# A GLA head's value projection and part of the modulation put between the level products' steps, with TensorE in source order there

## The chip, the cores and the metric

The kernel runs on one core of one Trainium2 chip, as one launch. The time is the device time of one execution in microseconds; three runs of the kernel before are given, and their median is the number to compare with. The engines are named as in the profile: PE (TensorE, the matrix products), DVE (VectorE), ACT (ScalarE), POOL (GpSimd) and SP (SyncE, which issues most DMAs). Each engine takes its own instructions strictly in the order in which the program lists them, and waits for the others by semaphores.

## The reference, cut to what matters

The reference is a trunk of four layers over 512 latent tokens and 256 context tokens with 1024 features. Each layer makes shift, scale and gate from a conditioning vector (the modulation, `s @ w_mod[i] + b_mod[i]`, 3072 columns), norms its tokens, runs a mixer, and adds the gated, normed result. Layers 0 and 3 have the mixer that the change touches, gated linear attention (GLA) with four heads, key width 128 and value width 256, in both directions:

```
for i in range(DEPTH):                       # kinds: GLA, window attention, RG-LRU, GLA
    shift, scale, gate = split(silu(c) @ w_mod[i] + b_mod[i], 3)
    h = rmsnorm(x, g_pre[i]) * (1 + scale) + shift
    q, k, v, z = split(h @ a_w_in[j])        # per head: 128, 128, 256, 256 columns
    # log gates of every token from a low-rank product; decays between tokens
    o = gla_bidir(q, k, v, la_f, la_b, s_f, s_b)
    y = (rmsnorm_head(o) * silu(z)) @ a_w_out[j]
    x = x + gate * rmsnorm(y, g_post[i])
```

Layer 3 leaves the context's output out, so its heads have fewer tokens in q, z and o.

## The kernel before, in words

Every fp32 product is made of three products of operands split in a high and a low part. Products of 256 or 512 columns run in PE back to back; their weights come in blocks of 256 columns through two 512 KB buffers (`raw`), which the modulation's weights use too, are split by ACT (L243) and by DVE or POOL (L246), and are one block ahead of their use (`weights`).

One GLA head goes through these steps in `gla`:

- `gates(h)`: four small products (L954) and then a chain on ACT and DVE (L958 to L970) that ends in `tmp` and `ls`, the exponentials of the gates' sums over blocks of 1, 2, 4 to 128 tokens. It needs the two PSUM pairs `sct` that the levels of the head before have used.
- `project(h)`: q and k (L362, 72 or 96 products), put into `q` and `Y` by ACT (L984, L979).
- `outputs` of the head before (`prev`): five steps of the state. `turn` transposes Y on PE (L1108), ACT and DVE split it (L1110, L1111), and `step` multiplies it with v (L1118, six products) and updates two states on DVE (L1131). Then chunk products in pairs (L1146), a norm (L1148 to L1152), and the transposed result (`give`, L1159). `turn`, `step`, `chunk` and `give` share two PSUM banks (`mxt`).
- `levels(h)`: X = tmp * q on DVE (L1012; there is one buffer X, so it waits for the last chunk product of the head before), then seven steps L = 1, 2, 4 to 64. Each step has 32 to 96 small products (L1035), 4 at a time beside each other, and behind them DVE decays halves of X and Y (L1063) and ACT copies parts of Y to K (L1030) for the next step. At the end DVE, ACT and POOL make the two score tiles A from the `sct` pairs (L1074 on).
- `zgates(h - 1)`: the gate z of the head before (L372; 48 products of 128x256 and 48 of 128x512 in layer 0, 48 of 128x512 in layer 3).
- `values(h)`: v in three pieces of 48 products of 128x256 (L349).
- `mods`: parts of the modulation, each a DMA of two `raw` buffers, eight products on PE (L499), and later a last step (L517 or L557).

Outside of a `manual_schedule` a scheduler orders every engine at compile time: each instruction has the priority of its place in the source, and the scheduler takes, by its own estimate of durations, the earliest one in the source that is ready. So what comes late in the source fills the times in which what comes early has to wait. Inside `tc.manual_schedule(engines=...)` the named engines keep the source's order among the instructions written there.

The order of one head in the source is: gates, project with outputs of the head before among it, three mods, levels with the z steps behind its steps 1, 3, 5 and 6, the rest of z, values, two mods.

Of the kernel before, what the change touches and what calls it, by code (L numbers as in the profile page):

```python
# [11 lines left out]
F32R = mybir.dt.float32r  # L12
# [63 lines left out]
def body(ctx: ExitStack, tc: tile.TileContext, I, out, layers=(0, 1, 2, 3)):  # L76
# [28 lines left out]
    @contextmanager  # L105
    def phase(name, single=2, double=2):
        """a phase's own SBUF pool and the PSUM banks that phases share out anew, singly and in pairs"""
        with ExitStack() as st:
            if open_already:
                st.push(open_already.pop())  # L110
            else:
                open_banks(st, name, single, double)
            yield open_pool(st, name, bufs=1)

# [10 lines left out]
    # the first phase's banks are there from the start  # L125
# [26 lines left out]
    # the RG-LRU's small parameters  # L152
# [7 lines left out]
    def lru_parameters(bank):  # L160
# [10 lines left out]
        # half biases for the gates' tanh form of the sigmoid  # L171
        V.tensor_scalar(hb, ps[:, 50:90], 0.5, None, op0=ALU.mult)
        # softplus(-lam) = max(-lam, 0) + ln(1 + exp(-|lam|)), times -4 and 2
# [13 lines left out]
    class Mixed:  # L187
        """the mixer's output, features on the partitions; its last two chunks' room is free for
        other use until they are written"""
# [31 lines left out]
    def loadw(pieces):  # L221
        """256 columns; what is returned takes them apart once they are there"""
        rs = []
        for k0 in range(0, KC, 4):
            r = raw()
            for src, o, n in pieces:
                nc.sync.dma_start(
                    r[:, :, o : o + n],
                    src[k0 * P : (k0 + 4) * P, :].rearrange("(k p) n -> p k n", p=P),
                )  # L230
            rs.append(r)

        def convert():
            wh = wp.tile([P, KC, 256], F32R, name="wh", tag="wh")
            wl = wp.tile([P, KC, 256], F32R, name="wl", tag="wl")
            for k0, r in zip((0, 4), rs):
                split(wh[:, k0 : k0 + 4, :], wl[:, k0 : k0 + 4, :], r)
            return wh, wl

        return convert  # L240
# [7 lines left out]
    def load_g1(a):  # L248
        """the low-rank gate projection, both directions, four times over along the columns"""
# [19 lines left out]
    def load_g2(a, zero=True, load=True):  # L269
        """three times over, each direction's rows against its own columns; gpt is free for it"""  # L270
# [16 lines left out]
    def plan(i):  # L287
        """the layer's weight blocks in the order of use"""
# [46 lines left out]
    def weights(key, ahead=True):  # L335
        """the next weight block, with the one after it on its way"""
# [7 lines left out]
    def passes(ps, a, b, kc):  # L344
        """ps += a^T b for pairs (hi, lo) of operand getters over the contraction chunks."""
# [8 lines left out]
    # products begun ahead of their use: the bank's part, and how many tokens of it are done  # L354
    begun = {}

    def ws_part(w, c0, ps, t0, n):
        """128 output columns on the partitions, tokens along the free axis"""
# [8 lines left out]
    def product_steps(ps, w, c0, t0, n):  # L367
        """the same, one product at a time; yields what each takes"""
# [9 lines left out]
    def ws(w, c0, stream):  # L378
        """128 output columns for all tokens of the stream"""
# [8 lines left out]
    def ws_ctx(w):  # L388
        """the context's tokens for both halves of the columns, in one bank but for what was begun elsewhere"""
# [11 lines left out]
    def begin(stream):  # L401
        """the first 256 tokens of what the next weight block brings first"""
# [11 lines left out]
    def ts(wk, kc, rk, tts, ps=None):  # L414
        """tokens on the partitions, 256 output columns along the free axis, for two token tiles."""
# [15 lines left out]
    def gate(pool, w, c0, stream, dst, parts=1):  # L431
        """dst (128 channels, the stream's tokens) *= silu(z), z a 128-column block of the projection."""
# [3 lines left out]
    def gate_ctx(pool, w, dst):  # L436
        """the same for both of the block's halves"""
        silu_times(pool, ws_ctx(w)[0], dst[:, :, CTX0:])
# [15 lines left out]
    def z_steps(pool, w, c, b, put, streams=("ctx", "lat")):  # L454
        """silu(z) for chunk b of the mixer's output, ahead of the output or behind it; put holds
        the token tiles of which either is there"""
# [48 lines left out]
    def mod_ss(i, n, bank, pool=None, bufs=1):  # L505
        """shift (n 0-3) and scale (n 4-7) of layer i, with the features on the partitions; in three steps."""
# [28 lines left out]
    def mod_gate(i, n, bank, pool=None, bufs=1):  # L535
        """gate * g_post of layer i, on all partitions; in three steps."""
# [34 lines left out]
    def background(n):  # L571
        """the next of the modulations; the last step of each comes with the one after it"""
# [20 lines left out]
    def unit_rstd(pool, x, xn):  # L593
        """1 / rms(x); xn is overwritten"""
# [4 lines left out]
    def unit(pool, x, xn):  # L599
        """xn = x / rms(x)"""  # L600
# [3 lines left out]
    def norm_part(pool, i, pr, xn, k, h=None):  # L604
        """xn: token tile -> x / rms(x); writes two chunks of h of layer i, transposed and split, to Rh / Rl."""
# [21 lines left out]
    def first_norm(i):  # L627
        """the same before the first layer, where the modulation comes late: x / rms(x) waits
        transposed in OG, and goes on as its chunks' shift and scale come in. A GLA's first
        products follow chunk by chunk."""  # L630
# [54 lines left out]
        # (two groups share a bank: the first one's first product clears the flags of both)  # L685
# [47 lines left out]
    def finish(i, kc, extra, last, final, xsrc, xdst):  # L733
        """out projection of OG, post norm, residual, and the next layer's pre norm."""
# [3 lines left out]
        with phase(f"fin{i}", 6, 0) as fp:  # L738
# [22 lines left out]
            def product(w, q, tt, ps, k0=0, k1=kc):  # L761
                """a quarter of the columns for a token tile"""
# [10 lines left out]
            def take(q, tt, ps):  # L773
                """quarters 0 and 1, then 2 and 3 at once"""
# [36 lines left out]
            def halves(*parts):  # L811
                """the second half of the columns, a quarter of a token tile at a time"""
# [36 lines left out]
            def chain(tt):  # L849
                """one step of a token tile's way to the next layer's operand at a time"""  # L850
# [64 lines left out]
    def gla(i, a, ctx_out):  # L915
# [3 lines left out]
        with phase(f"gla{i}") as mp:  # L919
# [16 lines left out]
            def gates(h):  # L936
                """exp of the log gates' sums over aligned blocks of 1, 2, .. 128 tokens;
                plane 0 is the backward direction, plane 1 the forward one."""
# [58 lines left out]
            def values(h, v):  # L997
                w = weights(f"v{h}")
                for pr in ((4, 5), (0, 1), (2, 3)):
# [7 lines left out]
            def levels(ls, q, Y, X, A):  # L1007
                """scores inside the 128-token chunks by halving; leaves in X and Y the operands
                decayed to the chunk's edges."""
# [86 lines left out]
            def outputs(h, X, Y, A, v, tl):  # L1096
                gh = mp.tile([P, GDV], F32, name="gh", tag="gh")
                nc.scalar.dma_start(gh, I["a_g_head"][a, h : h + 1].to_broadcast([P, GDV]))
                # the states in front of each chunk, forward (plane 0 of Y) and backward, side by side
# [100 lines left out]
            def mods(n):  # L1200
                for _ in range(n):
                    background(1)
                    yield

# [7 lines left out]
            def among(main, side, every, lead=0):  # L1212
                """steps of main with one of side after some of them; what main leaves of side"""
# [8 lines left out]
            for h in range(GH):  # L1222
# [8 lines left out]
                run(mods(3))  # L1231
                X = mp.tile([P, 2, T], F32, name="X", tag="X")
                A = [mp.tile([P, 6, P], F32R, name=n, tag=n) for n in ("Ah", "Al")]
                lv = levels(ls, q, Y, X, A)
                among(lv, z, [1, 3, 5, 6])
                run(z)
                # the lower part lies where the last head's output goes, but for that head's own
                if h < GH - 1:
                    OG.b = None
                    vl = OG.tail(F32R)  # L1240
                else:
                    vl = mp.tile([P, 2, T], F32R, name="vl", tag="tmp")
                v = (
                    mp.tile([P, 6, GDV], F32R, name="v", tag="v"),
                    vl.rearrange("p d t -> p (d t)").rearrange("p (c n) -> p c n", c=6),
                )
                run(values(h, v))
                run(mods(2))
# [6 lines left out]
    def attention(i):  # L1255
        with phase(f"att{i}", 6, 0) as mp:
# [12 lines left out]
            def rotate(x):  # L1269
                """axial rope on the latent tokens of x (two heads on the partitions), in place."""  # L1270
# [8 lines left out]
            def twice(x, e):  # L1279
                """head e of x on both halves of the partitions"""  # L1280
# [28 lines left out]
            def q_block(kv):  # L1309
                """q of four heads, each head's two parts stacked along the partitions, and their k  # L1310
                in two parts, each of them twice along the partitions"""
# [42 lines left out]
            def fill(ns):  # L1354
                """some of the projections' products, between those of the heads"""
# [13 lines left out]
            def scores(b, qt):  # L1369
# [3 lines left out]
                # local scores in a bank of each head; the context's behind them, in a bank  # L1373
                # of both heads where they do not fit
# [101 lines left out]
            # each unit's scores are a unit ahead of its transposes, two ahead of its output  # L1476
# [23 lines left out]
    def rglru(i, ex, mp):  # L1500
# [33 lines left out]
        def mix(b, up):  # L1534
# [19 lines left out]
            # planes: r', i' of the forward direction, then of the backward one  # L1554
# [24 lines left out]
            for d in range(2):  # L1579
                # sqrt(1 - a^2) = (1 + a) sqrt(tanh(y / 2)) with a = exp(-y)  # L1580
# [11 lines left out]
                # the scan writes over sqrt(1 - a^2), which x holds by now  # L1592
# [99 lines left out]
```

## Time and profile before

| | before |
|---|---|
| three runs, us | 1570.82, 1573.35, 1574.89 |
| median, us | 1573.35 |
| span of the profiled execution, first to last instruction, us | 1568.0 |
| instructions in it | 31484 |
| PE busy | 1489.2 us, 95% |
| DVE busy | 1040.6 us, 66% |
| ACT busy | 774.9 us, 49% |
| POOL busy | 289.1 us, 18% |

Of the profiled execution the profile gives the span, 1568.0 us; it has no time of its own beside that. The median of the three timed runs is 5.35 us above it. A busy time counts the union of an engine's instructions; the products of PE overlap in its pipeline, so a PE that is busy all the time may still have started its products further apart than it could.

GLA takes from 54 us to 377 us (layer 0) and from 1248 us to 1515 us (layer 3) of the span.

### The profile page before, as it was taken

What the parts mean: (1) busy time and instruction counts of PE and PEld (TensorE: products, weight loads), DVE (VectorE), ACT (ScalarE), POOL (GpSimd) and SP (SyncE); (2) the same over time, 40 slices, a digit from 0 to 9 for tenths busy, and PEclk for the clock granted to TensorE, in tenths of its full rate; (3) what the DMA queues carried; (4) which work ended last, traced back from release to release, by engine and by line L of the source; (5) the groups of instructions that cost most, each with busy time, mean ns of one, the idle gap of its engine ahead of it and who ended that gap; (6) DMA issues with size and microseconds to landing.
All of it is one profiled execution on the core that took longest, in us unless ns stands there. A gap on an engine that the chain in (4) does not pass through costs nothing.

```text
span 1568.0 us, 31484 instructions
## 1 busy us (share of the span) xinstructions
PE 1489.2 (95%) x12819; PEld 1279.1 (82%) x12819; DVE 1040.6 (66%) x1918; ACT 774.9 (49%) x1567; POOL 289.1 (18%) x338
## 2 busy tenths in 40 slices
PE   6989999999999999999999999899999999999998
PEld 3777788889987777788789877778899877878888
DVE  5586647575363388787872679989852675776753
ACT  5644343534252376565552556666742545454241
POOL 2221302112121200101001212222311311211211
PEclk8999999999999999999999999999999999999999
DMA  9432324113474532222134633222151243112132
GB/s 306 139 114 78 122 62 132 55 47 130 158 235 133 165 83 58 61 59 55 54 115 143 224 102 114 67 64 61 57 176 44 99 143 98 38 53 68 45 108 81
DMA packets 153057, 162.51 MB, mean 104 GB/s; under 512 B 12418, under 2 KB 141968, under 8 KB 152912
## 3 DMA queue, kind: packets, MB, share of 16 engines
q1 hardware_dynamic: 147456, 146.56, 30.6%
q10 hardware_dynamic: 5456, 13.94, 2.5%
q8 instruction: 101, 1.65, 0.4%
q14 instruction: 44, 0.36, 0.1%
HBM read 138.44 MB, written 11.53 MB: 96 GB/s over the span
## 4 chain that ended last, share of the span: by engine, by line
PE 49%; DVE 12%; ACT 5%; issue 4%; DMA 3%; POOL 1%; SPq 1%; POOLq 0%; ACTq 0%; DVEq 0%
PE mxt L768 16%; PE pjt L372 9%; PE pjt L362 5%; PE pjt L349 3%; PE mxt L1464 3%; PE mxt L1450 2%; PE mxt L499 2%; PE sct L1563 2%; DMA raw<-in_w_mod_dram 1%; PE mxt L1146 1%; PE mxt L1412 1%; PE mxt L1395 1%; DVE wl L246 1%; ACT wh L243 1%; DMA bb<-in_b_mod_dram 1%
## 5 line engine op out<-in xcount | busy, mean ns | idle before, releaser
L362 PE MATMUL pjt<-Rh,wh 128*128 128x256 f32 (+1 forms) x592 | 199.6, 338 | 8.8 <-DVE Rh L624 5.3
L768 PE MATMUL mxt<-wh,Rh 128*128 128x256 f32 x704 | 200.7, 285 | 0.0
L362 PE MATMUL pjt<-Rl,wh 128*128 128x256 f32 (+1 forms) x592 | 198.8, 336 | 1.9 <-DVE Rl L625 1.6
L768 PE MATMUL mxt<-wh,Rl 128*128 128x256 f32 x704 | 198.9, 283 | 0.0
L768 PE MATMUL mxt<-wl,Rh 128*128 128x256 f32 x704 | 198.9, 283 | 0.0
L362 PE MATMUL pjt<-Rh,wl 128*128 128x256 f32 (+1 forms) x592 | 197.5, 334 | 0.0
L243 ACT CAST wh<-raw 128x1024 fp32r<-128x1024 f32 x118 | 122.8, 1050 | 88.6 <-PE pjt L362 22.4
L372 PE MATMUL pjt<-Rl,wh 128*128 128x512 f32 (+1 forms) x448 | 161.1, 360 | 0.0
L372 PE MATMUL pjt<-Rh,wh 128*128 128x512 f32 (+1 forms) x448 | 160.4, 358 | 0.0
L372 PE MATMUL pjt<-Rh,wl 128*128 128x512 f32 (+1 forms) x448 | 159.0, 355 | 0.0
L246 POOL TENSOR_TENSOR wl<-raw,wh 128x1024 fp32r<-128x1024 f32 x32 | 85.5, 2670 | 304.0 <-ACT wh L243 232.6
L768 PEld LDWEIGHTS mxt<-wh,Rh 128*128 128x128 f32 x704 | 134.9, 192 | 1.9 <-issue 1.6
L768 PEld LDWEIGHTS mxt<-wh,Rl 128*128 128x128 f32 x704 | 134.7, 192 | 0.3 <-DVE Rl L751 0.2
L768 PEld LDWEIGHTS mxt<-wl,Rh 128*128 128x128 f32 x704 | 134.9, 192 | 0.1
L362 PEld LDWEIGHTS pjt<-Rh,wh 128*128 128x128 f32 x592 | 112.7, 191 | 24.5 <-DVE Rh L624 6.9
L246 DVE TENSOR_TENSOR wl<-raw,wh 128x1024 fp32r<-128x1024 f32 x86 | 110.4, 1289 | 33.1 <-ACT wh L243 32.8
L362 PEld LDWEIGHTS pjt<-Rl,wh 128*128 128x128 f32 x592 | 112.7, 191 | 16.4 <-DVE Rl L625 4.0
L349 PE MATMUL pjt<-wh,Rh 128*128 128x256 f32 x432 | 124.2, 287 | 0.0
L349 PE MATMUL pjt<-wl,Rh 128*128 128x256 f32 x432 | 123.9, 287 | 0.0
L349 PE MATMUL pjt<-wh,Rl 128*128 128x256 f32 x432 | 123.8, 286 | 0.0
L362 PEld LDWEIGHTS pjt<-Rh,wl 128*128 128x128 f32 x592 | 112.9, 191 | 13.0 <-issue 1.2
L777 DVE TENSOR_TENSOR y<-mxt,gpt 128x256 f32<-128x256 f32 (+1 forms) x66 | 33.6, 512 | 110.8 <-ACT y L776 110.8
(293 smaller groups left out, 3673.9 us busy)
## 6 DMA issues: line engine op xcount, KB each, us to landing
rawp<-in_w_mod_dram SPq DMA_DIRECT2D x48, 512.0 KB, 6.2
raw<-in_w_mod_dram SPq DMA_DIRECT2D x48, 512.0 KB, 3.6
raw<-in_a_w_in_dram SPq DMA_DIRECT2D x32, 512.0 KB, 3.5
raw<-in_b_w_in_dram SPq DMA_DIRECT2D x20, 512.0 KB, 4.6
raw<-in_c_w_in_dram SPq DMA_DIRECT2D x20, 512.0 KB, 3.6
xd<-x SPq DMA_DIRECT2D x18, 512.0 KB, 2.6
raw<-in_a_w_out_dram SPq DMA_DIRECT2D x16, 512.0 KB, 3.4
x<-xd ACTq DMA_DIRECT2D x16, 512.0 KB, 8.8
```

What stands on the lines that cost most here:

```text
L243: S.copy(h, x)
L246: e.tensor_tensor(l, x, h.bitcast(F32), op=ALU.subtract)
L349: PE.matmul(ps, a(u, k), b(v, k), start=(n == 0), stop=(n == 3 * kc - 1))
L362: PE.matmul(ps, w[u][:, k, c0 : c0 + P], R[v][:, k, t0 : t0 + n], start=(k == 0 and u + v == 0), stop=(k == KC - 1 and u == 1),)
L372: PE.matmul(ps, w[u][:, k, c0 : c0 + P], R[x][:, k, t0 : t0 + n], start=(k == 0 and u + x == 0), stop=(k == KC - 1 and u == 1),)
L499: PE.matmul(ps[32 * g : 32 * g + 32, 0:256], sT[:, k, :], r2[k // 4][:, k % 4, :], start=(k < 4), stop=(k >= 4), skip_group_check=True,)
L768: PE.matmul(ps, l[:, tt * P : (tt + 1) * P], r, start=(k == 0 and u + v == 0), stop=(k == kc - 1 and u == 1),)
L777: V.tensor_tensor(y[tt][:, cq], ps, gpt[:, 1 if tt >= 4 else 0, cq], op=ALU.mult)
L1146: PE.matmul(ps[:, n, :], l, r, start=(m == 0), stop=(m == len(tm) - 1))
L1450: PE.transpose(u[e][:, c * P : (c + 1) * P], ps[e][:, m * P : (m + 1) * P], ident)
L1464: PE.matmul(po[64 * e : 64 * e + 64, 0:P], v[:, t, 64 * kv : 64 * kv + 64], pt[:, e, m * P : (m + 1) * P], start=(m == 0), stop=(m == len( ...
L1563: PE.matmul(ps[:, t0 : t0 + nn], wg[a][:, n, :], x[c][:, p0 : p0 + nn], start=(q == 0), stop=(q == 2),)
```

## The change: what it does

`values` makes its own tiles, and is called as the tail of a side generator: first the z steps of the head before, then v. One side step comes behind each level step (for head 0, which has no z, behind steps 0, 2 and 4). One mod comes behind the level steps 0, 2, 4 and 6 (1, 3, 5 and 6 for head 0), in place of three ahead of the levels and two behind v; so a head has four instead of five, and the 13 of layer 0 reach into its last head. All of this stands in a `manual_schedule` for PE alone. Comments are taken out too, and line numbers from there on are higher by 10 (L1035 is L1045, L1108 is L1118, L1118 is L1128, L1146 is L1156, L1159 is L1169).

```
             def values(h, v):
                 w = weights(f"v{h}")
+                # the lower part lies where the last head's output goes, but for that head's own
+                if h < GH - 1:
+                    OG.b = None
+                    vl = OG.tail(F32R)
...
+                v += [
...
-            def mods(n):
-                for _ in range(n):
-                    background(1)
-                    yield
...
                 among(os, pr, [0, 3, 6], 2)
                 run(pr)
-                run(mods(3))
                 X = mp.tile([P, 2, T], F32, name="X", tag="X")
                 A = [mp.tile([P, 6, P], F32R, name=n, tag=n) for n in ("Ah", "Al")]
-                lv = levels(ls, q, Y, X, A)
-                among(lv, z, [1, 3, 5, 6])
-                run(z)
...
-                run(values(h, v))
-                run(mods(2))
+                v = []
+
+                def side():
+                    yield from z
+                    yield from values(h, v)
+
+                sd = side()
+                with tc.manual_schedule(engines={PE.engine}):
+                    for n, _ in enumerate(levels(ls, q, Y, X, A)):
+                        if n in ((0, 2, 4, 6) if prev else (1, 3, 5, 6)):
+                            background(1)
+                        if prev or n in (0, 2, 4):
+                            next(sd, None)
+                    run(sd)
                 prev = (h, X, Y, A, v, tl)
```

The first place is PE in layer 3, in the outputs of head 1 behind the projection of head 2. L1118 (L1128 in the changed kernel) are the products of a state step, L1108 (L1118) the transposes of the next, L372 the products of z, L1035 (L1045) small level products. Before:

```order
L1118 MATMUL mxt<-v,ktl 128x256
L372 MATMUL pjt<-Rh,wh 128x512
L372 MATMUL pjt<-Rl,wh 128x512
L372 MATMUL pjt<-Rh,wl 128x512
L372 MATMUL pjt<-Rh,wh 128x512
L1035 MATMUL sct<-q,Y 32x32 x2
L372 MATMUL pjt<-Rl,wh 128x512
L372 MATMUL pjt<-Rh,wl 128x512
L1108 MATMUL mxt<-ident,Y 128x128 x2
L372 MATMUL pjt<-Rh,wh 128x512
L372 MATMUL pjt<-Rl,wh 128x512
L1118 MATMUL mxt<-v,kth 128x256
```

And now, at the same place:

```order
L1128 MATMUL mxt<-v,ktl 128x256
L1045 MATMUL sct<-q,Y 32x32
L1118 MATMUL mxt<-ident,Y 128x128 x2
L1128 MATMUL mxt<-v,kth 128x256
L1128 MATMUL mxt<-OGb,kth 128x256
L1128 MATMUL mxt<-v,ktl 128x256
```

The products of z have gone from between the steps; none of them stands ahead of the first level's last product.

The second place is PE in layer 0, behind the gates' products of head 0. L362 is the projection, L169 a transpose of parameters, L349 are products of v, L499 those of a mod, L1035 (L1045) the first level's small products, which read X. Before:

```order
L362 MATMUL pjt<-Rl,wh 128x256
L362 MATMUL pjt<-Rh,wl 128x256
L169 MATMUL mxt<-ident,raw 128x110
L349 MATMUL pjt<-wh,Rh 128x256
L349 MATMUL pjt<-wl,Rh 128x256
L349 MATMUL pjt<-wh,Rl 128x256
L349 MATMUL pjt<-wh,Rh 128x256
L1035 MATMUL sct<-q,Y 32x32
L349 MATMUL pjt<-wl,Rh 128x256
L499 MATMUL mxt<-raw,sT 32x256 x4
```

And now:

```order
L362 MATMUL pjt<-Rh,wh 128x256
L362 MATMUL pjt<-Rl,wh 128x256
L362 MATMUL pjt<-Rh,wl 128x256
L1045 MATMUL sct<-q,Y 32x32
L1045 MATMUL sct<-X,Y 32x32
```

The products of v and of two mods, which stood ahead of the first level's products on X, stand behind them.

The third place is PE in the levels of that head, between the steps L = 2 and L = 4 of the changed kernel:

```order
L349 MATMUL pjt<-wl,Rh 128x256
L349 MATMUL pjt<-wh,Rl 128x256
L1045 MATMUL sct<-X,K 32x32 x24
L169 MATMUL mxt<-ident,raw 128x110
L1045 MATMUL sct<-X,K 32x32 x24
L349 MATMUL pjt<-wh,Rh 128x256
```

A third of v, 48 products, stands as one block on either side; between these two steps there is one transpose.

## Rows read from the trace of the kernel before

**Rows 1.** The page, busy time of each engine over the span.

```profile
PE 1489.2 (95%) x12819; PEld 1279.1 (82%) x12819; DVE 1040.6 (66%) x1918; ACT 774.9 (49%) x1567; POOL 289.1 (18%) x338
```

**Rows 2.** Stretches: length, then busy time and count by engine, PE's clock; both GLA layers.

```profile
core 0: us, PE busy (x) PEld busy (x) DVE busy (x) ACT busy (x) POOL busy (x), PEclk, DMA share, GB/s
66.15:377.00 310.85, 297.70 (x3385) 252.67 (x3384) 204.41 (x317) 137.13 (x247) 57.45 (x75) 0.99 0.29 88
1248.00:1514.60 266.60, 249.71 (x2506) 213.28 (x2506) 181.44 (x272) 124.98 (x215) 51.23 (x68) 1.00 0.23 69
```

**Rows 3.** Stretches: the output stages of two heads, and the sum of all six.

```profile
124.09:144.78 20.69, 19.29 (x130) 16.75 (x128) 10.63 (x25) 8.18 (x23) 2.74 (x6) 1.00 0.00 1
...
1380.05:1398.89 18.84, 17.19 (x105) 14.17 (x103) 10.92 (x22) 8.87 (x20) 1.35 (x4) 1.00 0.21 60
...
sum 116.46, PE 110.55 PEld 94.31 DVE 64.62 ACT 49.69 POOL 14.60; mean PE 18.42 PEld 15.72 DVE 10.77 ACT 8.28 POOL 2.43
```

**Rows 4.** The same stretches, PE on line L372 (z) alone.

```profile
124.09:144.78 20.69, 8.29 (x40) 5.82 (x40) 1.00 0.00 1
...
1380.05:1398.89 18.84, 8.62 (x29) 4.87 (x29) 1.00 0.21 60
...
sum 116.46, PE 52.20 PEld 33.44; mean PE 8.70 PEld 5.57
```

**Rows 5.** Timeline, outputs of head 1 in layer 3: start, duration, engine, line, idle before.

```profile
1382.50 1.00 ACT L979 COPY Y<-pjt 128x1024 f32<-128x1024 f32 x1
1383.56 0.31 PE L1035 MATMUL sct<-q,Y 128*32 128x32 f32 x4 [1.62 <-ACT Y L979]
1385.15 0.40 ACT L1110 CAST kth<-mxt 128x256 fp32r<-128x256 f32 x1
1385.31 1.23 DVE L246 TENSOR_TENSOR wl<-raw,wh 128x1024 fp32r<-128x1024 f32 x1 [0.52 <-ACT wh L243]
1386.45 0.87 DVE L1131 SCALAR_TENSOR_TENSOR st<-st,tl,mxt 128x256 f32<-128x256 f32 x2
1387.24 0.42 DVE L1111 TENSOR_TENSOR ktl<-mxt,kth 128x256 fp32r<-128x256 f32 x1
1387.98 0.36 PE L1118 MATMUL mxt<-v,kth 128*128 128x256 f32 x1
...
1397.44 1.22 DVE L1012 TENSOR_TENSOR X<-tmp,q 128x1024 f32<-128x1024 f32 x1
```

**Rows 6.** Timeline, level step L = 2 of head 2 in layer 3.

```profile
1402.68 0.79 ACT L1030 COPY K<-Y 128x256 f32<-128x256 f32 x2 [1.41 <-DVE Y L1063]
1403.19 0.66 PE L1035 MATMUL sct<-X,K 128*32 128x32 f32 x32 [0.92 <-ACT K L1030]
1403.78 0.51 PE L372 MATMUL pjt<-Rl,wh 128*128 128x512 f32 x1
1404.13 0.39 PE L372 MATMUL pjt<-Rh,wl 128*128 128x512 f32 x1
1404.35 0.39 PE L372 MATMUL pjt<-Rh,wh 128*128 128x512 f32 x1
```

**Rows 7.** Timeline, gates of head 0 in layer 0.

```profile
64.59 0.61 PE L954 MATMUL sct<-t,g 96*128 96x256 f32 x2
70.97 1.28 ACT L176 ACT_TABLE_LOAD   x1
72.80 1.28 ACT L177 ACT_TABLE_LOAD   x1
77.60 1.75 DVE L1012 TENSOR_TENSOR X<-tmp,q 128x1536 f32<-128x1536 f32 x1
```

**Rows 8.** Stretches: v of head 1 in layer 0; around a long wait of PE.

```profile
171.65:190.93 19.28, 19.28 (x164) 17.97 (x162) 11.40 (x15) 5.08 (x8) 8.79 (x11) 1.00 0.22 67
81.00:89.60 8.60, 4.67 (x56) 4.40 (x45) 7.80 (x9) 3.93 (x6) 3.39 (x2) 0.90 0.37 113
89.60:94.70 5.10, 5.09 (x110) 4.70 (x111) 3.14 (x4) 2.01 (x5) 0.00 (x0) 0.50 0.15 50
```

**Rows 9.** DMA issues of the modulation's weights: count, size, median us to landing.

```profile
raw<-in_w_mod_dram SPq DMA_DIRECT2D x48, 512.0 KB, 3.6
```

More of the change, by code (lines that the diff above doesn't have):

```diff
@@ L998, in values @@
                 w = weights(f"v{h}")
+                if h < GH - 1:
+                    OG.b = None
+                    vl = OG.tail(F32R)
+                else:
+                    vl = mp.tile([P, 2, T], F32R, name="vl", tag="tmp")
+                v += [
+                    mp.tile([P, 6, GDV], F32R, name="v", tag="v"),
+                    vl.rearrange("p d t -> p (d t)").rearrange("p (c n) -> p c n", c=6),
+                ]
                 for pr in ((4, 5), (0, 1), (2, 3)):
@@ L1230, in gla @@
                 run(pr)
-                run(mods(3))
                 X = mp.tile([P, 2, T], F32, name="X", tag="X")
                 A = [mp.tile([P, 6, P], F32R, name=n, tag=n) for n in ("Ah", "Al")]
-                lv = levels(ls, q, Y, X, A)
-                among(lv, z, [1, 3, 5, 6])
-                run(z)
[L1238 to L1246, printed above, removed]
-                run(values(h, v))
-                run(mods(2))
+                v = []
[10 more added lines that the diff above has]
+                    run(sd)
                 prev = (h, X, Y, A, v, tl)
```

## The prediction, made before the changed kernel ran

> **What bounds the kernel now.** I read the page first: PE is busy for 95% of the span [rows 1], so what counts is the time in which PE starts nothing. Then the two GLA stretches: PE is idle for 310.85 - 297.70 = 13.2 us in layer 0 and for 266.60 - 249.71 = 16.9 us in layer 3 [rows 2]. These 30 us are all that the change could take away as waits. Then I looked at where GLA would leave PE without work, and what covers it there. The largest cover is in the outputs of the head before: from the first state step to the first level's products on X these six stages take 116.46 us, PE is idle for only 116.46 - 110.55 = 5.9 us of them, and 52.2 us of its busy time are products of z [rows 3, 4].
>
> Why z stands there is seen in one round of the states [rows 5]. A transpose on PE is copied by ACT (0.40), split by DVE (0.42), and multiplied by PE; DVE then updates two states (0.87) before the PSUM bank is free again. With a split of weights (1.23) in between on DVE, the state products start at 1387.98, 0.3 us after their operand is there (1387.24 + 0.42). So z did not hold the chain up; it filled it. At the end X can be made (1.22 us from 1397.44) only when the last chunk product has read the old X, and the levels wait for it.
>
> **The change part by part.** The operations stay the same ones; their order on PE changes, and with it what PE can do while it waits.
>
> *Output stages of heads 1 to 3, both layers.* In the changed order no product of z stands ahead of the first level's last product, and v stands behind z; nothing else is left for PE there. The chain on ACT and DVE is the same. So the stage keeps its length and what z filled becomes a wait. Upper bound: all of 52.2 us plus the 5.9 us of today, 58 us [rows 3, 4]. Lower bound: z's busy time counts overlap. Two products of 512 columns start 0.22 us apart (1404.13 to 1404.35 [rows 6]), those of 256 columns about 0.12 us (164 products, 144 of them of v, in 19.28 us [rows 8]). Each of the three stages of layer 3 holds 29 of 512 columns [rows 4], 6.5 us; for layer 0's 127, some of either kind, I count 0.12 each, 15 us. Sum 19.5 + 15 + 5.9 = 40 us. I take 50. In layer 3 I add 5 us for the three: there v now ends before the last two level steps, the gates of the next head wait for the score tiles to leave PSUM, and fall into the second half of the projection; their exponentials then stand on ACT between the copies of the state steps. That makes 55 us of idle PE (bounds 40 to 60).
>
> *Head 0 of layer 0.* Today's 14 us between the gates' products (64.59) and the end of X (77.60 + 1.75 = 79.35 [rows 7]) are filled with v and two mods. Now PE has about 1 us of projection, and then the level products, which wait for X, with everything behind them in line. The chain gets shorter by what leaves ACT: parameters and their two table loads (2 x 1.28 [rows 7]) and a mod's copy now come later, about 4 us. I take a wait of 10 us (bounds 8 to 14), 2 us more between those level steps that have only a mod or a transpose between them, and 2 us for the clock behind the wait. 14 us.
>
> *Head 0 of layer 3.* The projection ends just before the levels, so the first wait is short; steps without a piece of v between them wait about 1 us each, as today's step does (0.92 [rows 6]). 3 us.
>
> *Level steps of the other six heads.* Between two steps there are now 24 to 48 full products, 2.9 to 5.8 us, so waits for K and for the decays, like today's 0.92 us [rows 6], are covered. A new one comes: in layer 0 the second mod of a head needs two weight buffers, which the v block holds until its split is done; SP issues the mod's DMA behind that, and it lands 3.6 us later [rows 9], while PE, in source order, stands at the mod. I take 2 us for heads 1 and 2, and 2 us for small waits of all heads. 6 us.
>
> *Fewer changes between small and full products.* A full product behind small ones starts its successor 0.35 us later (1403.78 to 1404.13) instead of 0.22 [rows 6]. In the program's order z stands in about 16 pieces per head today, from now on in 2 or 4; at 0.13 us, and some more for mods that are cut in pieces, that gives back about 10 us over six heads. Head 0 of layer 0 gives back its clock: behind a wait of PE of some 4 us its 5.1 us from 89.60 ran at half the granted clock [rows 8], worth 2.5 us.
>
> *The sum.* Idle PE in GLA: 55 + 14 + 3 + 6 = 78 us, against 30 us today, +48; less 10 and 2.5: +35 us. All else (the attention and RG-LRU layers, the output projections) keeps its order in substance. Against the profiled span, 1568.0 + 35 = 1603; the median of the three runs lies 5.35 us above the span, so I predict 1608 us, 2.2% slower.
>
> **The clock.** PE's granted clock is 1.00 through the output stages today [rows 3]; after a wait of some 4 us in head 0 of layer 0 it fell to 0.50 of 2.4 GHz, and came back with the products that followed [rows 8]. The new stages are idle for almost half their time, though in pieces of 0.5 to 2 us. The Trainium skill, "TensorE: Matmul & The Clock Gate", section "What's actually happening", says that the low clock is the default state and that activity releases it. By that rule the stages could lose the clock; by the rows, waits of 1 to 2 us (1.62 in rows 5) did not cost it.
>
> **The rivals.**
> - *The clock falls in most of the new waits.* For it: the half of the stage that is idle. Against it: no single wait there is as long as the one of 4 us. Price: what the one fall cost, 2.5 us, in six or seven stages, and it hits the chunk products, on which the chain waits: +16 us, 1624 us.
> - *The stages shrink in part.* If DVE and ACT, which no longer take z's parts there and whose weight splits (1.23 each [rows 5]) may slide out from between the steps, turn a round faster, each stage loses 3 to 4 us: -20 us, 1587 us. Against it: each round passes PE, ACT, DVE and DVE again, and its parts are not shared.
> - *The covered level steps win: faster.* The place is the same six stages. The change breaks even when their idle time is about 20 us instead of 55, a stage of 13 us instead of 19; at 12 us each, 1568 us. For it: PE's own work in a stage is only about 10 us (18.84 - 8.62 [rows 3, 4]). Against it: one round of the states, from ACT's copy at 1385.15 to the end of the split at 1387.66, takes 2.5 us without PE [rows 5], there are five, and X comes only behind the chunk products that follow. I see only one way there: that the rounds were held up by PE, and rows 5 say no.
>
> **How the numbers follow.** The forecast as such 0.56, with its own range 1596 to 1620; the clock 0.16; the shrunken stages 0.18; faster or no change, 0.10 together. A difference under 0.3% can't be told from none here (the three runs spread by 0.26%). Slower by over 0.3%: 0.90; within it: 0.03; faster: 0.07. The range takes in the shrunken stages (1587) and most of the clock's case: 1582 to 1636.
>
> **What would show it.** Right: PE idle in the two GLA stretches near 80 us instead of 30; in the six output stages no L372 product, lengths of 17 to 21 us, and waits of PE there for DVE's split, for the states and for X, near 8 to 9 us a stage; a wait of about 10 us for X in head 0 of layer 0; no wait over 0.5 us between level steps that have z or v between them; some wait for `raw` at the second mod in heads 1 and 2. Wrong: output stages well under 17 us; a PE idle sum near 30; or a time lost outside GLA.

## The result, and the profile after

The changed kernel takes 1638.78 us (median; 1636.64 to 1639.08) against 1573.35 us for the kernel before: a ratio of 1.042, 95% interval 1.0398 to 1.0442. A fourth execution of the kernel before took 5019.49 us and is left out of both. The direction was forecast, the size was not: 35 us were predicted on the profiled span, and it grew by 69.2 us, from 1568.0 to 1637.2. In the line numbers of the changed kernel everything from `values` on stands ten lower down: the small level products are L1045, the copies K L1040, X L1022, the transposes of a state step L1118, its halves kth and ktl L1120 and L1121, its products L1128, the states st L1139 and L1141, the chunk products L1156.

The first view is the page's busy time, to be held against [rows 1].

```profile
PE 1505.9 (92%) x12819; PEld 1299.1 (79%) x12819; DVE 1044.9 (64%) x1918; ACT 774.5 (47%) x1567; POOL 278.7 (17%) x338
```

The same 12819 products are busy 16.7 us longer. Where, the stretches tell; these two begin and end at the same places as those of [rows 2], to within 0.4 us (columns as there).

```profile
65.36:413.07 347.71, 301.63 (x3388) 261.06 (x3387) 206.54 (x317) 137.48 (x248) 56.22 (x75) 0.93 0.25 77
1282.34:1580.64 298.30, 263.73 (x2496) 225.28 (x2495) 178.22 (x268) 123.35 (x212) 51.07 (x68) 0.92 0.20 62
sum 646.01, PE 565.36 PEld 486.34 DVE 384.77 ACT 260.83 POOL 107.29; mean PE 282.68 PEld 243.17 DVE 192.38 ACT 130.42 POOL 53.65
```

All of the loss is here: 646.01 against 577.45 us is 68.6. PE is idle for 80.65 us (30 before) and busy for 565.36 (547.41 before), and its clock is 0.93 and 0.92 on average instead of 0.99 and 1.00. So 50.6 us are waits, and by 18.0 us PE's busy time has grown.

The six output stages answer to [rows 3]; on L372, z, they have 0.00 (x0) each, against 52.20 us in [rows 4].

```profile
130.17:155.99 25.82, 17.71 (x85) 15.08 (x85) 12.26 (x28) 9.26 (x23) 2.67 (x5) 0.74 0.00 1
228.80:246.68 17.88, 13.76 (x85) 11.20 (x85) 9.44 (x20) 6.08 (x21) 2.65 (x5) 1.00 0.00 1
315.63:333.52 17.89, 13.78 (x85) 11.20 (x85) 9.45 (x20) 6.08 (x21) 2.65 (x5) 1.00 0.00 1
1354.06:1374.74 20.68, 15.17 (x70) 12.60 (x70) 10.97 (x25) 8.47 (x20) 1.26 (x3) 0.67 0.22 68
1427.61:1447.93 20.32, 14.27 (x70) 11.68 (x70) 12.30 (x27) 9.12 (x19) 1.24 (x3) 0.75 0.18 52
1500.74:1521.57 20.83, 14.90 (x71) 12.49 (x71) 12.31 (x27) 10.06 (x21) 1.24 (x3) 0.75 0.17 50
sum 123.42, PE 89.59 PEld 74.25 DVE 66.73 ACT 49.08 POOL 11.71; mean PE 14.93 PEld 12.37 DVE 11.12 ACT 8.18 POOL 1.95
```

They are 7 us longer in sum than before, though z is gone from them, and four of the six lost the clock. Where one of them loses it is seen in a timeline of PE in the second output stage of layer 3 (start, duration, line, idle before and its releaser); it answers to [rows 5].

```profile
1427.95 0.28 PE L1128 MATMUL mxt<-v,ktl 128*128 128x256 f32 x1
1428.07 0.28 PE L1128 MATMUL mxt<-v,kth 128*128 128x256 f32 x1
...
1429.32 0.44 PE L1118 MATMUL mxt<-ident,Y 128*128 128x128 f32 x2 [0.56 <-ACT st L1139]
1432.84 0.58 PE L1128 MATMUL mxt<-v,kth 128*128 128x256 f32 x1 [3.07 <-DVE ktl L1121]
1433.21 0.41 PE L1128 MATMUL mxt<-OGb,kth 128*128 128x256 f32 x1
1433.43 0.42 PE L1128 MATMUL mxt<-v,ktl 128*128 128x256 f32 x1
1433.64 0.42 PE L1128 MATMUL mxt<-v,kth 128*128 128x256 f32 x1
```

Ahead of the wait two products of 256 columns start 0.12 us apart, behind it 0.21. The wait itself is ACT's: the next head's gates stand there between two copies of the state steps.

```profile
1429.29 1.28 ACT L966 ACT_TABLE_LOAD   x1
1430.58 1.48 ACT L966 ACTIVATE tmp<-tmp 128x1536 f32<-128x1536 f32 x1
1431.97 0.63 ACT L1120 CAST kth<-mxt 128x256 fp32r<-128x256 f32 x2
```

The waits of PE, by releaser (us in total, times, longest), from the gates of head 0 on; first layer 0, then layer 3.

```profile
PE sct L1045 <- DVE X L1022: 17.6, 4, 13.3
PE mxt L499 <- DMA raw<-in_w_mod_dram: 7.4, 4, 3.6
PE sct L1045 <- ACT Y L979: 4.2, 1, 4.2
PE mxt L1128 <- DVE st L1141: 4.1, 6, 0.8
PE mxt L1128 <- DVE ktl L1121: 3.9, 4, 3.2
```

```profile
PE mxt L1128 <- DVE ktl L1121: 11.3, 5, 3.1
PE sct L1045 <- ACT Y L979: 4.4, 2, 2.6
PE mxt L1118 <- DVE st L1141: 3.9, 4, 1.0
PE sct L954 <- DVE ml L1089: 3.6, 2, 1.8
PE mxt L499 <- DMA raw<-in_w_mod_dram: 2.2, 1, 2.2
```

Three kinds are to be told apart: the chain of the state steps (ktl, st), as forecast; head 0's X and the mods' raw, as forecast; and waits at the seam from one head's levels to the outputs that follow (the gates for ml, and ktl ahead of a stage's first state product), which were not.

### The profile page after: what moved, and what is told of

Same layout as the page of the kernel before. It is cut to its first block, busy times and chain, and to the rows that moved or that the text cites. A ratio compares the mean times of both kernels' runs of the same rounds, so it can differ in the third digit from the quotient of the medians.

```text
span 1637.2 us, 31483 instructions
## 1 busy us (share of the span) xinstructions
PE 1505.9 (92%) x12819; PEld 1299.1 (79%) x12819; DVE 1044.9 (64%) x1918; ACT 774.5 (47%) x1567; POOL 278.7 (17%) x338
## 5 line engine op out<-in xcount | busy, mean ns | idle before, releaser
L362 PE MATMUL pjt<-Rh,wh 128*128 128x256 f32 (+1 forms) x592 | 200.9, 341 | 7.7 <-DVE Rh L624 5.3
L362 PE MATMUL pjt<-Rl,wh 128*128 128x256 f32 (+1 forms) x592 | 199.5, 338 | 1.8 <-DVE Rl L625 1.7
L362 PE MATMUL pjt<-Rh,wl 128*128 128x256 f32 (+1 forms) x592 | 198.7, 336 | 0.0
L372 PE MATMUL pjt<-Rh,wh 128*128 128x512 f32 (+1 forms) x448 | 161.8, 361 | 0.0
L372 PE MATMUL pjt<-Rl,wh 128*128 128x512 f32 (+1 forms) x448 | 159.4, 356 | 0.0
L372 PE MATMUL pjt<-Rh,wl 128*128 128x512 f32 (+1 forms) x448 | 158.9, 355 | 0.0
L362 PEld LDWEIGHTS pjt<-Rh,wh 128*128 128x128 f32 x592 | 113.7, 193 | 24.7 <-DVE Rh L624 6.9
L362 PEld LDWEIGHTS pjt<-Rl,wh 128*128 128x128 f32 x592 | 113.9, 193 | 15.5 <-DVE Rl L625 3.6
L349 PE MATMUL pjt<-wh,Rh 128*128 128x256 f32 x432 | 126.1, 292 | 0.0
L362 PEld LDWEIGHTS pjt<-Rh,wl 128*128 128x128 f32 x592 | 113.9, 193 | 12.2 <-issue 0.4
L349 PE MATMUL pjt<-wh,Rl 128*128 128x256 f32 x432 | 123.3, 285 | 0.0
L349 PE MATMUL pjt<-wl,Rh 128*128 128x256 f32 x432 | 123.3, 285 | 0.0
```

What stands on the lines that cost most here:

```text
L349: PE.matmul(ps, a(u, k), b(v, k), start=(n == 0), stop=(n == 3 * kc - 1))
L362: PE.matmul(ps, w[u][:, k, c0 : c0 + P], R[v][:, k, t0 : t0 + n], start=(k == 0 and u + v == 0), stop=(k == KC - 1 and u == 1),)
L372: PE.matmul(ps, w[u][:, k, c0 : c0 + P], R[x][:, k, t0 : t0 + n], start=(k == 0 and u + x == 0), stop=(k == KC - 1 and u == 1),)
```

## The experiments

Theories at the start: *cover* (z's place costs the waits), *order* or *v's place* (what stands between and behind the level steps costs), *the clock*. The kernel before was timed again beside them: 1572.02 us for *z put back*, *the order freed*, the 64 unread products and *head 0 alone*; 1569.68 for the 32 unread products, *the mods taken out*, *z alone* and *v alone*; 1570.83 for the last. Ratios are to these; they differ from the quotients of the medians by up to 0.001.

**z put back, v and the mods left between the steps.** In the head loop:

```
-                    yield from z
                     yield from values(h, v)
...
+                run(z)
                 with tc.manual_schedule(engines={PE.engine}):
```

> Edit: in the changed kernel z is emitted ahead of the block in which TensorE keeps source order; only v and the mods stand between the level steps. Theory 'cover' (z gone from the six output stages is what costs): the stages get z back as filling, PE's idle sum in the two GLA stretches falls from 82 us to 40 to 50, what stays is the wait for X in head 0 of layer 0 (13.3 us) and small waits for raw; 1580 to 1595 us. Theory 'order' (PE in source order through the level steps is what costs, wherever z stands): at least 1620 us.

1590.98 us, ratio 1.0126 (1.0106 to 1.0146), where *cover* put it: with z back, 46 us of the loss are gone by the two ratios. PE's idle sum in the two stretches is 50.3 us, just above the 40 to 50 expected. The largest waits left in layer 0 and in layer 3:

```profile
PE sct L1045 <- DVE X L1022: 13.3, 1, 13.3
PE mxt L1118 <- ACT st L1139: 4.6, 3, 4.3
PE mxt L499 <- DMA raw<-in_w_mod_dram: 3.4, 4, 1.4
...
PE sct L1045 <- DVE Y L1073: 5.6, 4, 1.7
PE mxt L1118 <- ACT st L1139: 4.7, 3, 1.6
```

**The order freed.** The block that keeps TensorE in source order is taken out, the code between the steps stays.

```
-                with tc.manual_schedule(engines={PE.engine}):
+                if True:
```

> Edit: in the changed kernel the block that keeps TensorE in source order is taken away; z, v and the mods stand between the level steps in the code as before, but the scheduler may pull them ahead. Theory 'cover': most of z goes back into the output stages, and v and the mods into head 0's wait for X; 1570 to 1590 us, PE's idle sum about 30 to 40 us. Theory 'queues' (the later issue of the mods' DMAs and weight splits, which stays as in the changed kernel, is what costs): over 1615 us.

1589.71 us, 1.012 (1.0103 to 1.0137), at the top of what *cover* gave: z went back into the stages, but 18 us stayed lost. The scheduler goes by the order of the code, where v now comes ahead of the last steps. Its waits in layer 3 are at the seam again:

```profile
PE mxt L1128 <- DVE ktl L1121: 6.7, 4, 2.4
PE sct L954 <- DVE ml L1089: 3.6, 2, 1.8
```

**Products that nobody reads, in z's old place.** Ahead of the levels of heads 1 to 3:

```
+                for _ in range(4 if prev else 0):
+                    ps = pjt()
+                    for k in range(16):
+                        PE.matmul(ps[:, :256], Rh[:, k % KC, 0:128], Rh[:, k % KC, 0:256],
+                                  start=(k == 0), stop=(k == 15))
```

> Edit: the changed kernel with 64 products of 128x256 on Rh whose result nobody reads, ahead of the levels of each head but the first; they fall between the state steps, chunk products and transposes of the six output stages, about 7 us a stage, where z stood before. Theory 'clock' (the fall of the granted clock in these stages is a large part of the loss): the granted clock stays at 1.00 there, the products of the stages run at full speed, and the time falls by 10 to 25 us to 1615 to 1628 although 42 us of work were added. Theory 'waits alone': the clock's fall costs nothing since the chain on ACT and DVE sets the stages' length; 1639 us or up to 20 us more.

1634.28 us, 1.0401 (1.0384 to 1.0419): between the two, so it settles nothing by itself. In layer 0, 28 of a stage's 64 products came behind the last chunk products and were paid for in full (its second and third stage grew from 17.9 to 20.9 us). So I halved the dose (`range(16)` to `range(8)`), which ends ahead of the last chunk products.

> Edit: as the kernel with 64 products nobody reads, with 32 for each of the six output stages, so that they end before the last chunk products and add some 4 us of work a stage, all of it in waits. Theory 'the clock is on the path': products of the changed kernel at half clock took some 25 us longer in the two GLA stretches than their like at full clock; where the clock holds, 15 to 20 us come back, 1619 to 1626 us. Theory 'the clock is absorbed' (the chain on ACT and DVE sets the length of the stages): within 6 us of the 1634 us that 64 products gave.

1628.96 us, 1.0383 (1.0358 to 1.0409); the profiled span fell by 9.1 us. That lies where *the clock is absorbed* put it, at its lower edge. The two GLA stretches, from the gates of head 0 to the last product of z in layer 3, and in layer 0 to some 3.5 us before z's end (all products, then those that nobody reads):

```profile
64.06:406.28 342.22, 304.54 (x3479) 268.06 (x3479) 201.21 (x314) 135.54 (x243) 56.29 (x75) 0.95 0.26 81
1285.88:1571.15 285.27, 263.31 (x2555) 225.61 (x2556) 173.51 (x260) 118.51 (x203) 48.48 (x65) 0.97 0.21 65
sum 627.49, PE 567.86 PEld 493.67 DVE 374.71 ACT 254.05 POOL 104.77; mean PE 283.93 PEld 246.83 DVE 187.36 ACT 127.02 POOL 52.39
```

```profile
sum 627.49, PE 31.93 PEld 27.59; mean PE 15.96 PEld 13.80
```

The same stretches of the changed kernel and of the kernel before, in this order:

```profile
sum 638.57, PE 558.24 PEld 480.15 DVE 377.41 ACT 254.24 POOL 104.63; mean PE 279.12 PEld 240.07 DVE 188.70 ACT 127.12 POOL 52.32
```

```profile
sum 570.01, PE 540.55 PEld 460.03 DVE 378.50 ACT 255.51 POOL 106.30; mean PE 270.27 PEld 230.02 DVE 189.25 ACT 127.76 POOL 53.15
```

The clock was held only in part: 0.95 and 0.97, against 0.93 and 0.92 in the changed kernel and 0.99 and 1.00 before. By the trace's records of the clock it is low for 51 us of these stretches, in the changed kernel for 92, before for 7. The kernel's own products, without the unread ones, are busy for 545.4 us in the trace. (To take 31.93 from 567.86 would give 535.9, which is too little, since the two kinds overlap in the pipeline.) That is 12.8 us less than in the changed kernel, and 4.9 more than before. The time falls by 638.57 - 627.49 = 11.1 us, so for the part of the clock that this run gave back, nearly all shows in the length. What the other low stretches cost, this run can't say. Two stages of layer 3, which took 20.32 and 20.83 us, now kept the clock:

```profile
1422.87:1441.25 18.38, 15.34 (x101) 12.95 (x101) 12.31 (x27) 9.98 (x21) 1.24 (x3) 1.00 0.20 58
1494.06:1512.44 18.38, 15.32 (x101) 12.92 (x101) 12.31 (x27) 9.96 (x21) 1.24 (x3) 1.00 0.18 58
```

**Head 0 alone scheduled freely.**

```
-                with tc.manual_schedule(engines={PE.engine}):
+                with tc.manual_schedule(engines={PE.engine}) if prev else ExitStack():
```

> Edit: the changed kernel with TensorE in source order only for heads 1 to 3 of the two GLA layers; head 0 of each is scheduled freely. Theory 'cover, and head 0 apart': the wait of 13.3 us for X in head 0 of layer 0 and the low clock behind it go, v and the mods fill it: 13 to 20 us less, 1619 to 1626 us; the six output stages keep their lengths. If head 0's wait only puts off work that is waited for later: within 5 us of 1639.

1628.13 us, 1.0363 (1.034 to 1.0385): some 9 us less than the changed kernel by the two ratios, 14.2 by the two spans. The wait for X is gone (the longest one left for it in layer 0 is 1.4 us). That is nearest to *head 0 apart*: by the median 2 us above its range.

**The mods taken out of the steps**: `background(3)` ahead of the levels and `background(2)` behind v instead of one at a time between the steps.

> Edit: the changed kernel with the mods out of the level steps: three are emitted ahead of the levels and two behind v, for the scheduler to place; z and v stand between the steps in source order. Theory 'the mods' transfers hold PE in source order': the waits for raw (7.4 us in layer 0, 2.2 us in layer 3) go, and three mods fill part of head 0's wait for X: 1622 to 1630 us. Theory 'they only fill': without them the steps wait as long for K and the decays, 1636 us or more.

1642.74 us, 1.0473 (1.0442 to 1.0503), no gain, rather a loss. X's longest wait fell to 2.4 us, but the mods still wait, for 5.6 us in layer 0 against 7.4:

```profile
PE sct L1045 <- DVE X L1022: 6.6, 4, 2.4
PE mxt L499 <- DMA raw<-in_w_mod_dram: 5.6, 5, 2.6
```

So it is not source order alone that makes them wait for raw; what sets the time of that transfer I did not separate further.

**z alone between the steps**; v behind them, mods as before (their two lines are not shown).

```
-                    yield from values(h, v)
...
                     run(sd)
+                run(values(h, v))
```

> Edit: z alone stands between the level steps in source order; v behind the levels and the mods ahead and behind as in the kernel before. Theory 'cover': z's place alone costs the waits and the low clock of the six output stages, 35 to 50 us, 1607 to 1622 us. Theory 'v's place' (v moved forward leaves the chain from the scores to the next head's gates uncovered): most of the loss stays away, under 1595 us.

1622.30 us, 1.0344 (1.0313 to 1.0375): 52.6 us slower than before, at the very top of *cover*. With the first experiment (v and mods alone: 19.0) this makes 71.6 us, a little over the 65.4 us of the whole change; by the spans it is 48.4 and 19.4, against 69.2. The two parts nearly add in sum, though not head by head, as the table below shows.

**v alone, in the middle heads.** z ahead of the levels and v between the first steps for heads 1 and 2 only, mods as before:

```
+                if h in (1, 2):
+                    run(z)
+                    with tc.manual_schedule(engines={PE.engine}):
+                        among(lv, values(h, v), [0, 1, 2])
...
```

> Edit: only v of heads 1 and 2 of each GLA layer stands between the first four level steps in source order; z is emitted ahead of them and fills the output stages; heads 0 and 3 and all mods are as in the kernel before. Heads 1 and 2 took 0.2 to 2.6 us less each where z stood ahead (stage start to stage start against before). Theory 'the level steps alone gain from v': 1 to 5 us faster than before, 1567 to 1571 us. Theory 'v behind the levels covers the next head's gates': slower than before by 2 to 6 us.

1586.26 us, 1.0114 (1.0095 to 1.0134). Slower, and by more than *v behind the levels covers* asked for, but not for its reason: layer 3 lost nothing (260.17 us against 260.56), layer 0 lost some 20. There the three mods were placed in the output stages (48 of their products in a stage of 38.7 us), and v then waited for its weights:

```profile
PE pjt L349 <- POOL wl L246: 4.0, 2, 2.3
...
PE pjt L349 <- DVE wl L246: 2.2, 2, 1.7
```

**The same with the mods in the steps**, four for each of heads 1 and 2; heads 0 and 3 as in the kernel before.

```
+                        for n, _ in enumerate(lv):
+                            if n in (0, 2, 4, 6):
+                                background(1)
+                            next(sd, None)
```

> Edit: heads 0 and 3 of each GLA layer are as in the kernel before (z among the levels for the scheduler to place, v and two mods behind them, three mods ahead); in heads 1 and 2 z is emitted ahead of the levels, and between the level steps stand v and four mods in source order. Where all heads stood so, the stretches from output stage to output stage behind heads 1 and 2 took 84.7 and 78.6 us in layer 0 against 87.3 and 80.0 us before, 62.2 and 62.7 against 62.4 and 63.2 us in layer 3; head 0 lost 6.9 and 1.5 us and the last head 9 and 6 us. Theory 'ends only' (all the loss that z's return left was in heads 0 and 3): 1 to 5 us faster than before, 1567 to 1571 us on this chip. Theory 'weights' (with z ahead and v between the first steps v's split weights and the mods' transfers come too late): 5 to 15 us slower than before, as in the run where v alone was moved in these heads.

1567.80 us, ratio 0.9981 (0.9967 to 0.9995): 3 us less than before, in the range of *ends only*. No other version is faster than the kernel before, and this one by less than the 0.3% that the prediction counts as a difference; the two profiled spans are both 1568.0 us. In the table, heads 1 and 2 of layer 0 gain 9.5 us in this run (head 1 with one mod less, which stands in head 2), and head 3 and layers 1 and 2 lose 10.3. Why layers 1 and 2 take longer in this run and in the one with v and the mods alone, no run shows.

The profiles of these runs as one table: us from the gates of head 0 to the first state step of stage 1, from stage to stage, and from the last head's first state step to the first product of the output projection (layer 3: to the program's last product).

| stretch | before | after | z only | v, mods only | middle heads |
|---|---|---|---|---|---|
| layer 0, head 0 | 60.3 | 67.2 | 60.0 | 67.5 | 60.4 |
| head 1 | 87.3 | 98.6 | 96.1 | 84.7 | 79.5 |
| head 2 | 80.0 | 86.8 | 87.2 | 78.6 | 78.3 |
| head 3 | 56.7 | 66.8 | 69.6 | 65.8 | 60.5 |
| last outputs | 28.8 | 30.1 | 28.8 | 26.2 | 28.8 |
| layers 1, 2 | 876.8 | 875.4 | 876.6 | 882.4 | 883.3 |
| layer 3, head 0 | 64.0 | 66.1 | 63.8 | 65.5 | 64.6 |
| head 1 | 62.4 | 73.6 | 69.2 | 62.2 | 61.8 |
| head 2 | 63.2 | 73.1 | 70.6 | 62.7 | 62.7 |
| head 3 | 50.1 | 62.7 | 56.8 | 56.4 | 50.3 |
| last outputs, end | 67.7 | 66.8 | 67.6 | 65.6 | 67.6 |

z's column loses in heads 1 to 3 of both layers, 49.9 us in sum. v's is longer in heads 0 and 3 (24.1 us) and shorter in heads 1 and 2 (4.7 us), where z in the stage and the products of the next head's projection stand beside the chain. In heads 3 of v's column PE does not wait more. These are the stretches of the two heads 3 in that run, then in the kernel before (columns as in [rows 2]):

```profile
293.69:359.44 65.75, 65.36 (x798) 58.19 (x799) 45.21 (x69) 24.13 (x49) 10.04 (x11) 1.00 0.22 68
1458.38:1514.82 56.44, 53.01 (x563) 44.99 (x562) 39.37 (x60) 25.49 (x47) 8.85 (x7) 1.00 0.19 59
```

```profile
291.38:348.03 56.65, 55.34 (x730) 49.58 (x728) 38.49 (x57) 20.00 (x46) 13.24 (x18) 1.00 0.13 41
1443.21:1493.29 50.08, 46.37 (x535) 40.27 (x534) 33.52 (x53) 18.51 (x40) 8.65 (x15) 1.00 0.15 47
```

PE is idle for 0.4 and 3.4 us there, against 1.3 and 3.7 before. The stretches are longer because z came forward into them: 162 and 84 of its products (L372) instead of 108 and 55, and 16 of a mod (L499) in layer 0. These products are missing behind, in the last outputs: in layer 0 that stretch lost 54 of its 84 products of z, but only 2.6 us of its length, and PE is idle for 4.7 us of it instead of 0.4.

## Why the prediction fell short

**Right.** No product of z is left in the stages. Five of the six lengths lie in 17 to 21 us. X is waited for 13.31 us in head 0 of layer 0 (10 taken, bounds 8 to 14); head 0 costs 6.9 us more there and 2.0 in layer 3. The second mod waits for raw in layer 0 (3.55 us in head 1). Between the level steps of heads 1 to 3 no wait for K or for the decays over 0.2 us is left. The gates' exponentials fall between ACT's copies in layer 3. Nothing is lost outside GLA. The idle sum was to be near 80 us and is 80.65.

**The idle sum is right by errors that cancel.** In the stages idle time is 123.42 - 89.59 = 33.8 us and not 55 (5.6 a stage, not 8 to 9), in part because products at half the clock fill it; elsewhere it is 80.65 - 33.8 = 46.8 us and not 23. And the busy time, from which 10 and 2.5 us were to go, grew by 18.0. So the sum has to be judged by place. The six stages are 7.0 us longer than before, where 5 us were added. Without them the two stretches take 646.01 - 123.42 = 522.6 us; the forecast comes to 577.45 + 35.5 - 116.46 - 5 = 491.5. So 31 us are missing outside the stages, and 24 of them are idle time there (46.8 instead of 23).

**The step that failed most: the waits outside the stages, "14 + 3 + 6".** In the two heads 0 the 17 us are 17.4 + 7.2 = 24.6. For the other six heads the 6 us are 22.2: 6.5 us of waits for raw (2 taken), and 13.4 us at the seam, of which nothing stood in the sum outside the stages: 6.6 for ktl ahead of a stage's first state product, 3.6 for ml at the gates, 3.2 for Y and ktl in the last head of layer 3. "Waits for K and for the decays ... are covered" came true of the level steps. But v and two mods had also stood behind the last step, over the chain from the scores to the next gates and the first state step. I had moved v and asked only what it would cover at its new place.

The experiments agree in sum. Against the 24 us that are idle outside the stages today, and with the 2.5 us of the clock, v's and the mods' part of the change was to cost -3.7 us. Alone it cost 19.4 us, on top of z's part 1637.2 - 1616.4 = 20.8 (spans). Where it costs depends on z. On top of z's part it is 9.4 us in heads 0, 12.8 in heads 1 to 3 of layer 3 and nothing in those of layer 0 (-0.6). With z in its place, heads 1 and 2 don't need v behind the levels (4.7 us gained). In heads 3 v's early place let the last z come forward, and the last outputs stood without cover; with these heads put back, in the last run, z stands as before (108 and 55 products), and heads 3 lose 3.8 us in layer 0 and 0.3 in layer 3.

**The second: the clock, "-2.5", and a rival of 0.16.** z's part was to cost 55 - 5.9 - 10 = 39 us and cost 48.4. Instead of giving 2.5 us back, the clock was low for 92 us of the two stretches, against 7 before. The run with 32 unread products took 41 us of that away, and with it 12.8 us of busy time and 11.1 of length; what the rest costs no run shows. Nor does any run show the 10 us for *fewer changes between small and full products* by themselves. Pieces of z and v that stand right behind small products are 35 instead of 64 in the two layers, which at the prediction's 0.13 us gives 3.8, an estimate; the pieces of mods are not in it.

I had held the clock safe since no single wait was to be as long as the 4 us of [rows 8]. Waits near that size came: 4.24 us for Y in head 1 of layer 0, 3.07 and 3.08 for ktl in layer 3, the very wait for which I added 5 us there. But the longest wait does not decide alone. With z alone between the steps the third stage of layer 0 lost the clock, too, though its longest wait is 1.55 us:

```profile
306.47:329.66 23.19, 17.21 (x88) 14.55 (x86) 10.61 (x21) 8.04 (x23) 5.00 (x6) 0.78 0.16 46
```

In the changed kernel the stages at 1.00 have waits of at most 1.42 us, and behind one of them, from 333.52 to 339.00, the clock is 0.69. The Trainium skill, "TensorE: Matmul & The Clock Gate", section "What's actually happening", makes the low clock the default that activity releases. The four stages agree with it, at 0.67 to 0.75 behind waits of 2.60 to 4.24 us; what tells them from the two at 1.00 no run shows by itself.

So of the 34 us that are missing on the span, 23 lie in v's and the mods' part and 9 in z's, by the two experiments. How much of either is the clock stays open: holding it in part gave back 11.1 us in GLA, 9.1 on the span, and by the medians' ratios, whose intervals overlap, 6.

**Rivals.** The clock's rival, 1624 us, named something that did happen, but priced it at 16 us and alone; the waits outside the stages were missed beside it. The stages did not shrink as a whole: two lost 3 us or 0.9 against before, four grew. That the covered level steps win is seen only where z stays in its place: 2.6, 1.4, 0.2 and 0.5 us for the four middle heads (the first with one mod less, the second with one more).

## What to carry to other kernels

Work that a scheduler has drawn into a stage where PE waits for a chain on other engines is that stage's cover; before moving it, ask what else PE has there, and also what the work that is moved stood in front of at its old place. If a move makes new waits among sparse products, price the clock on top of them, and do not take waits of 1.5 us for safe: here some of them kept the clock and some lost it. When an idle forecast comes out right, compare its parts as well, since slow products and waits can stand in for each other.

## Not expected of the hardware

Two stages with the same 85 products had waits of at most 1.42 us and kept a granted clock of 1.00, though behind one of them it fell; four with a wait of 2.60 to 4.24 us fell to 0.67 to 0.75; and in another run a stage whose longest wait was 1.55 us fell to 0.78. At half the clock, state products of 256 columns start 0.21 us apart instead of 0.12. Thirty-two products that nobody reads, put into two such stages, shortened them from 20.3 and 20.8 us to 18.4; two stages that had the clock already grew by them from 17.9 to 18.2 and 18.1.
